# A list scheduler that makes gate products and table making own their destination slot first

## The chip, the cores and the metric

The kernel runs on the 8 cores of one Trainium2 chip. The metric is the device time of the slowest core, in microseconds (us). Most executions of one kernel agree within 0.3% (fast runs). There is a second, slower state, in which the cores of one die show a lower granted TensorE clock; such runs are called slow and are left out of every comparison here.

PE is TensorE's matmuls, PEld its weight loads, DVE is VectorE, ACT is ScalarE, POOL is GpSimd and SP is SyncE.

## The reference

One inference step of a 4-layer decoder trunk, on 8 prompts of 2048 tokens and 128 single-token samples. Cut to what matters:

```python
def _layer(x, ...):
    h = rmsnorm(x);  z = h @ w_in                 # zb, zc, zv, zu, ga, gs
    conv_out, _ = conv_causal(zc * zv, ...)       # "convolution products": zc, zv, zb
    ya = zb * conv_out
    ys, hr, hi = s5(zu, ...)                      # diagonal state-space scan
    gy = gelu(ys)
    ys = gy * sigmoid(gy @ w_glu + b_glu)         # "GLU products"
    m = sigmoid(ga) * (ya @ wb1) + sigmoid(gs) * (ys @ wb2)   # "gate products": ga, gs
    x = x + m @ w_out
    x = x + (silu(h2 @ w_gate) * (h2 @ w_up)) @ w_down
```

Each core takes one prompt, in two halves, and a share of the samples. The scan is done with tables of powers of the state's eigenvalues, in four scan groups per layer. The tables are made on DVE, ScalarE and GpSimd while the first half of a layer is being worked on. The second half loads the saved tables. Making a table is a long chain of elementwise work with two sines in it.

## The kernel before

Nothing is scheduled on the chip. A Python list scheduler with a model of the five engines fixes each engine's instruction order beforehand. Tiles live in pools of few slots; the pools that matter here are:

```python
    PP = Pool("psum", 8, lambda s: PSUM[s], reserve=3)        # the eight PSUM banks
    TP = Pool("tb", 4, lambda s: TB[:, s, :], reserve=-1)     # "TB rows": sigmoid(gate); also scratch of table making
    TABP = Pool("tab", 2, lambda s: TAB[:, s, :], reserve=-1) # a finished scan table
```

An operation may be picked when its inputs are ready and when every tile that it uses has a slot, or can get one:

```python
        def feasible(o, t):
            need = {}
            for tl in o.tiles:               # every tile that a read or write key of o names
                if tl.slot is None:
                    need.setdefault(tl.pool, []).append(tl)
            for p, tls in need.items():
                free = p.free
                if len(free) < len(tls):
                    return False
                ...                          # reserve, and turns in order for reserve=-1
            return True
```

A gate product is eight matmuls into a PSUM bank; a ScalarE sigmoid then empties the bank into a TB row:

```python
        def gas(j4):
            uga = [next_unit("ga") for _ in range(2)]
            for jj in range(4):
                t_ = tj[jj] = TP.new()
                for blk in blks:
                    pg = projh(uga[jj // 2], jj % 2, blk)      # takes a PSUM bank
                    act(lambda e, ...: e.activation(out=t_[...], in_=pg[...], func=AF.Sigmoid),
                        [(pg,)], [(t_, blk.i)], blk.n, tset="sig")   # takes the TB row
```

Here lies what the change is about. The product names only the bank. So it can run, and fill a bank, while the row that the sigmoid needs is still held by table making. Then the bank is blocked until the row is free.

## Time and profile before

| | before |
|---|---|
| time, median of 3 runs | 3663.6 us (3660.78 to 3669.47) |
| profiled span, slowest core | 3663.7 us (cores 3647.5 to 3663.7) |
| PE busy | 3504.0 us, 96% |

PE is busy for 96% of the span and carries 88% of the chain. A reordering can only win back PE's idle time, about 160 us. Only the first two slices, one in the middle and the last fall below nine tenths. The stretches table of the slowest core (busy us of each engine, instruction counts in brackets, then granted clock, DMA share, GB/s) shows where:

```profile
...
core 3: us, PE busy (x) PEld busy (x) DVE busy (x) ACT busy (x) POOL busy (x), PEclk, DMA share, GB/s
...
90.00:140.00 50.00, 20.57 (x244) 13.31 (x246) 45.44 (x67) 18.29 (x34) 15.32 (x13) 0.65 0.35 101
140.00:160.00 20.00, 19.09 (x322) 14.58 (x316) 8.42 (x13) 17.01 (x30) 4.35 (x5) 0.85 0.54 81
160.00:200.00 40.00, 39.42 (x392) 26.59 (x393) 25.07 (x57) 15.70 (x33) 2.11 (x4) 1.00 0.63 141
...
```

From 90 to 140 us, in layer 0's first half, PE works 20.57 of 50 us and DVE 45.44. The reading of that hole comes from PE's timeline (start, length, group; in square brackets the idle time before it and what ended it). L669 with H is a projection such as a gate product, L895 and L908 belong to table making, L1080 begins a scan group's output products, L1033 begins a scan group, and L669 with R at 195 us are the GLU products:

```profile
...
91.44 1.46 PE L669 MATMUL ps<-H,RING 128*128 128x384 bf16 x8
...
95.43 1.46 PE L669 MATMUL ps<-H,RING 128*128 128x384 bf16 x8
...
106.94 0.58 PE L895 MATMUL ps<-IDB,SC 128*128 128x128 bf16 x4 [5.79 <-ACT TAB L775]
...
111.34 2.72 PE L669 MATMUL ps<-H,RING 128*128 128x384 bf16 x8
...
128.63 0.58 PE L895 MATMUL ps<-IDB,SC 128*128 128x128 bf16 x4 [5.96 <-ACT R L775]
...
140.61 0.27 PE L1080 MATMUL ps<-UU,TAB 128*128 128x128 bf16 x1
...
160.14 0.67 PE L1033 MATMUL ps<-UU,TAB 128*64 128x64 bf16 x31
...
195.26 0.98 PE L669 MATMUL ps<-R,RING 128*128 128x384 bf16 x5
```

and ScalarE's timeline (L1158 is a gate's sigmoid, L775 and L776 are the two sines of a table):

```profile
...
137.80 1.28 ACT L1158 ACT_TABLE_LOAD   x1
139.09 1.93 ACT L1158 ACTIVATE TB<-ps 128x384 f32<-128x384 f32 x5
...
149.07 0.42 ACT L775 ACTIVATE TAB<-SC 128x256 f32<-128x256 f32 x1
...
155.84 1.49 ACT L1158 ACTIVATE TB<-ps 128x272 f32<-128x272 f32 x4
157.34 1.28 ACT L776 ACT_TABLE_LOAD   x1
158.64 0.51 ACT L776 ACTIVATE TAB<-SC,CST 128x256 f32<-128x256 f32 x1
...
```

Between the last of the sigmoids here (they end at 157.33) and the second sine (158.64) ScalarE runs an ACT_TABLE_LOAD of 1.28 us; the switch took about 1.30 us in all.

Five gate products run at 91.44, 95.43, 98.8, 99.7 and 111.34 us (the third and the fourth are in lines left out). All five sigmoids run in one group at 139.09, just after table making gave up the rows. So five of the eight banks lay blocked for 26 to 46 us. What else needed PE in that time (the convolution products, scan group 1's output products) waited for banks. Three banks were left, and often free, but `reserve=3` (in the lines of `feasible` left out above) keeps the last three for the tile whose turn it is in the program, and that was one of table making or of the scan. A rerun of the scheduler shows these products refused with three banks free. So five blocked banks closed PSUM to all other work. The group at 111.34 also shows the clock: eight matmuls took 2.72 us there, against 1.46 for the same product at 91.44. A gap of 5.79 us ends at 106.94, not 5 us ahead of the slow product; the clock record of this core drops to half at 104.85 us, inside that gap, and stays there until 145.81, so that the mean granted clock of this stretch is 0.65.

### The profile page before, as it was taken

Reading aid. Unit: us, or ns where it says so; the run is one execution under the profiler, and the core shown is the slowest. Engines: PE = TensorE matmul, PEld = TensorE weight load, DVE = VectorE, ACT = ScalarE, POOL = GpSimd, SP = SyncE. Lnnn points to the kernel's source line nnn. Section 1 sums busy time; section 2 is a strip of 40 time slices with the busy share of each in tenths; the row PEclk is TensorE's granted clock in tenths of the full one; section 3 lists DMA queues with packets and bytes.
Section 4 is the critical chain, followed back from the end, with each engine's and each line's share of the span. In section 5 each row is a group of like instructions: output and inputs, shape, how many; then the busy total and the mean of one; then the engine's idle time right before and its main releaser. Section 6 shows DMA issues by size and latency. Waiting matters only on the chain.

```text
span 3663.7 us, 67385 instructions; the slowest of 8 cores (3647.5 to 3663.7 us)
## 1 busy us (share of the span) xinstructions
PE 3504.0 (96%) x23912; PEld 1979.7 (54%) x23912; DVE 1618.6 (44%) x2889; ACT 1141.7 (31%) x2151; POOL 608.7 (17%) x799
## 2 busy tenths in 40 slices
PE   6699999999999999999999899999999999999998
PEld 3466666666666666666664344444444444444443
DVE  8745555465454654543244331354224442254313
ACT  4443234332353322533134320243103421042202
POOL 4232210322103221030000200002000110002000
PEclk9799999999999999999999999999999999999999
DMA  7444557435574355854338544574445644474443
GB/s 157 115 82 70 114 139 149 87 66 113 138 155 86 62 113 135 185 110 84 70 71 196 116 77 71 98 169 74 75 77 115 144 70 81 70 146 79 79 72 87
DMA packets 252804, 384.14 MB, mean 105 GB/s; under 512 B 157632, under 2 KB 180800, under 8 KB 246848
## 3 DMA queue, kind: packets, MB, share of 16 engines
q0 software_dynamic: 67968, 243.30, 39.5%
q1 hardware_dynamic: 184512, 136.53, 12.8%
q8 instruction: 202, 3.31, 0.4%
q14 instruction: 122, 1.00, 0.1%
HBM read 567.06 MB, written 56.12 MB: 170 GB/s over the span
## 4 chain that ended last, share of the span: by engine, by line
PE 88%; DVE 4%; issue 3%; DMA 3%; ACT 1%; SPq 1%; DVEq 0%; ACTq 0%; POOL 0%; POOLq 0%
PE ps L669 83%; DMA yT<-X 1%; PE ps L702 1%; PE ps L1107 1%; DVE SC L561 1%; DVE H L726 1%; PE ps L1033 1%; PE ps L908 1%; PE ps L1080 0%; DVE X L1246 0%; DMA scv<-CIN 0%; SPq L632 0%; PE ps L895 0%; DMA X<-xsT 0%; DVE R L1225 0%
## 5 line engine op out<-in xcount | busy, mean ns | idle before, releaser
L669 PE MATMUL ps<-H,RING 128*128 128x512 bf16 (+2 forms) x12160 | 2194.9, 340 | 23.5 <-DVE H L726 9.7
L669 PEld LDWEIGHTS ps<-H,RING 128*128 128x128 bf16 x12160 | 1191.5, 99 | 965.9 <-issue 52.3
L669 PE MATMUL ps<-R,RING 128*128 128x384 bf16 (+2 forms) x6400 | 1162.1, 339 | 19.7 <-DMA R<-dy 11.4
L669 PEld LDWEIGHTS ps<-R,RING 128*128 128x128 bf16 x6400 | 624.2, 98 | 517.8 <-issue 35.4
L656 POOL DMA_DIRECT2D RING<-wpk x472 | 253.0, 537 | 2635.0 <-PE ps L669 2431.7
L1268 DVE TENSOR_TENSOR R<-SC,ps 128x384 bf16<-128x384 f32 (+2 forms) x440 | 255.8, 583 | 786.7 <-PE ps L669 773.6
L1267 ACT ACTIVATE SC<-ps 128x384 f32<-128x384 f32 (+2 forms) x440 | 226.1, 515 | 1208.0 <-PE ps L669 1199.6
L1246 DVE TENSOR_TENSOR X<-X,ps 128x384 f32<-128x384 f32 (+2 forms) x480 | 269.8, 582 | 448.2 <-PE ps L669 445.2
L700 ACT ACTIVATE H<-X 128x384 bf16<-128x384 f32 (+2 forms) x304 | 156.6, 539 | 198.4 <-DVE X L1246 178.7
L726 DVE SCALAR_TENSOR_TENSOR H<-X,PRM,SC 128x384 bf16<-128x384 f32 (+2 forms) x304 | 183.0, 672 | 35.0 <-ACT SC L707 34.8
L1240 POOL TENSOR_TENSOR R<-TB,SC 128x384 bf16<-128x384 f32 (+1 forms) x160 | 168.1, 1063 | 113.1 <-DVE SC L1237 101.4
L1237 DVE TENSOR_TENSOR SC<-SC,ps 128x384 f32<-128x384 f32 (+1 forms) x160 | 92.7, 584 | 163.5 <-PE ps L669 78.6
L1236 ACT ACTIVATE SC<-ps 128x384 f32<-128x384 f32 (+1 forms) x160 | 81.4, 515 | 248.2 <-PE ps L669 219.8
L1213 DVE TENSOR_TENSOR TB<-TB,ps 128x384 f32<-128x384 f32 (+2 forms) x160 | 89.9, 582 | 128.6 <-PE ps L669 124.6
L1172 DVE TENSOR_TENSOR CIN<-ps,SC 128x384 f32<-128x384 f32 (+2 forms) x80 | 47.0, 587 | 200.7 <-ACT SC L1171 192.6
L561 DVE TENSOR_TENSOR SC<-TB 128x512 f32<-128x512 f32 (+1 forms) x160 | 124.1, 785 | 8.1 <-PE ps L908 0.6
L1158 ACT ACTIVATE TB<-ps 128x384 f32<-128x384 f32 (+1 forms) x160 | 78.9, 516 | 85.8 <-PE ps L669 85.4
L702 PE MATMUL ps<-H,ONESB 128*128 128x384 bf16 (+2 forms) x320 | 78.1, 348 | 27.5 <-ACT H L700 26.8
L561 POOL TENSOR_TENSOR TB<-TB 128x512 f32<-128x512 f32 (+1 forms) x72 | 89.3, 1242 | 42.3 <-DVE R L835 20.7
L1225 DVE TENSOR_TENSOR R<-R,SC 128x384 bf16<-128x384 bf16 (+2 forms) x80 | 46.4, 588 | 88.8 <-ACT SC L1223 86.7
L899 ACT ACTIVATE TAB<-ps 128x512 bf16<-128x512 f32 x60 | 35.5, 597 | 133.0 <-PE ps L895 132.8
L1171 ACT ACTIVATE SC<-ps 128x384 f32<-128x384 f32 (+2 forms) x80 | 41.0, 513 | 95.7 <-PE ps L669 95.5
(180 smaller groups left out, 1633.1 us busy)
## 6 DMA issues: line engine op xcount, KB each, us to landing
RING<-wpk POOLq DMA_DIRECT2D x440, 512.0 KB, 7.0
TAB<-stash SPq DMA_DIRECT2D x21, 1792.0 KB, 10.0
stash<-TAB SPq DMA_DIRECT2D x15, 1792.0 KB, 7.6
R<-stash SPq DMA_DIRECT2D x7, 1792.0 KB, 14.8
RING<-wpk POOLq DMA_DIRECT2D x32, 384.0 KB, 6.1
du<-R SPq DMA_DIRECT2D x32, 256.0 KB, 9.2
UU<-du SPq DMA_DIRECT2D x32, 256.0 KB, 7.2
dy<-YY SPq DMA_DIRECT2D x32, 256.0 KB, 6.6
```

Source lines behind the costliest of these rows:

```text
L561: fn = lambda e: e.tensor_tensor(out=out(), in0=a(), in1=b(), op=op)
L656: S.dma("pool", lambda e: e.dma_start(out=t[:, 0:n], in_=wpk[l, ui, :, 0:n]), [("X",) + gate] if gate else (), [(t,)], 128 * n * 4, prio=- ...
L669: subs.append((lambda e, u=u, kw=kw, c=c, src=src, i=i: e.matmul(ps[:, 0:blk.n], lhsT=u.ap(kw, c), rhs=src(blk), start=(i == 0), stop=(i = ...
L700: act(lambda e, kt=kt: e.activation(out=hq(kt), in_=xin(kt)[0], func=AF.Square), xin(kt)[1], qkeys(kt, blk), n)
L702: S.pe([(lambda e, kt=kt: e.matmul(ps[:, 0:n], lhsT=ONESB[:], rhs=hq(kt), start=(kt == 0), stop=(kt == 7)), qkeys(kt, blk) + [C_("ONESB")] ...
L726: dve(lambda e, kt=kt, xi=xi, g=g: e.scalar_tensor_tensor(out=H[:, kt, blk.c0:blk.c0 + n], in0=xi(), scalar=g, in1=rs[:, 0:n], op0=ALU.mul ...
L1213: dve(lambda e, po=po, n=n, t_=t_, blk=blk: e.tensor_tensor(out=t_[:, blk.c0:blk.c0 + n], in0=t_[:, blk.c0:blk.c0 + n], in1=po[:, 0:n], op ...
L1237: dve(lambda e, sg=sg, po=po, n=n: e.tensor_tensor(out=sg[:, 0:n], in0=sg[:, 0:n], in1=po[:, 0:n], op=ALU.mult), [(sg,), (po,)], [(sg,)], n)
L1240: S.op(MENG, lambda e, sg=sg, n=n, t_=t_, blk=blk, j=j: e.tensor_tensor(out=R[:, MT[j], blk.c0:blk.c0 + n], in0=t_[:, blk.c0:blk.c0 + n], ...
L1246: dve(lambda e: e.tensor_tensor(out=X[:, j, blk.c0:blk.c0 + n], in0=X[:, j, blk.c0:blk.c0 + n], in1=ps[:, 0:n], op=ALU.add), [(ps,)] + xke ...
L1267: act(lambda e, sg=sg, pg=pg, n=n: e.activation(out=sg[:, 0:n], in_=pg[:, 0:n], func=AF.Silu), [(pg,)], [(sg,)], n, tset="silu")
L1268: dve(lambda e, sg=sg, pu=pu, n=n, blk=blk, ti=ti: e.tensor_tensor(out=R[:, ti, blk.c0:blk.c0 + n], in0=sg[:, 0:n], in1=pu[:, 0:n], op=ALU ...
```

## The change

The gate product and the first DVE multiply of a table get an extra read key on their destination tile. Nothing ever writes that key, so it makes no dependence, no semaphore and no wait on the chip. It only makes the tile one of the operation's tiles, so that `feasible` asks for the TB row (or TAB slot) before the operation may take a bank (or scratch).

```diff
-    def proj(parts, blk):
+    def proj(parts, blk, own=()):
...
-                [u.key] + keys(blk), MMN(blk.n)))
+                [u.key] + keys(blk) + list(own), MMN(blk.n)))
...
-    def projh(u, mt, blk):
-        return proj([...], blk)
+    def projh(u, mt, blk, own=()):
+        return proj([...], blk, own)
...
-                tt(zz1, ..., ALU.mult, bkk, [(z1,)], 512)
+                tt(zz1, ..., ALU.mult, bkk + [(tab, "own")], [(z1,)], 512)
...
-                    pg = projh(uga[jj // 2], jj % 2, blk)
+                    pg = projh(uga[jj // 2], jj % 2, blk, [(t_, "own")])
```

More of the change, by code (lines that the diff above doesn't have):

```diff
@@ L79 @@
     LAT = 0.07
+    LATPE = 0.07
     SWITCH = 1.28
@@ L332, in schedule @@
                 s.npred -= 1
-                r = o.end + (0.0 if e == "pe" and s.eng == "pe" else self.LAT) - s.offs[i]
+                r = o.end + (0.0 if e == "pe" and s.eng == "pe" else self.LATPE if s.eng == "pe" else self.LAT) - s.offs[i]
                 if r > s.ready:
@@ L685, in rk @@
         return lambda blk: rkeys(t, blk)
-    def projh(u, mt, blk):
-        return proj([(u, k, mt * 128, hsrc(k), hk(k)) for k in range(8)], blk)
+    def projh(u, mt, blk, own=()):
+        return proj([(u, k, mt * 128, hsrc(k), hk(k)) for k in range(8)], blk, own)
     def projr(u, c, slots, blk):
@@ L864, in prep_f @@
                 o8 = 8 * h
-                tt(zz1, lambda: Bv(me, 0), lambda o8=o8: Pv(pw, o8), ALU.mult, bkk, [(z1,)], 512)
+                tt(zz1, lambda: Bv(me, 0), lambda o8=o8: Pv(pw, o8), ALU.mult, bkk + [(tab, "own")], [(z1,)], 512)
                 tt(zz2, lambda: Bv(bct, 256), lambda o8=o8: Pv(me, 512 + o8), ALU.mult, bkk, [(z2,)], 512)
```

## The prediction

> **What bounds the kernel now.** TensorE. The page shows PE busy 3504 of 3663.7 us (96%), granted clock 0.98, and PE as 88% of the chain that ended last. PE idles some 160 us in all, the bound for any reordering. The largest hole (stretches table): in 90 to 140 us PE is busy 20.6 of 50 us, while DVE is busy 45.4 (making layer 0's scan tables).
>
> **What the change does.** It adds no work and no wait on the chip. A list scheduler orders the kernel beforehand; the "own" key makes an operation eligible only once its destination slot (a TB row for a gate product, a TAB slot for a table's first multiply) is free. Only order changes.
>
> **Where it acts.** I matched each of 160 gate products in the trace with the ScalarE sigmoid that empties its bank. Long holds occur twice:
> 1. Layer 0, first half: five gate products run at 91.4 to 114 us, their sigmoids at 139.1 to 141.0, because table making holds all four TB rows until 137 to 140. Five of eight PSUM banks lie blocked 26 to 46 us each.
> 2. Second half's start: eight gate products at 1955.8 to 1969.7 hold all banks until 1974.5 to 1978 (PE idle 5.5 us). Rows are late because output stores are (yT<-X took 17 to 19 us to land), which the scheduler doesn't foresee: its plan has the rows free. I expect no change there.
>
> For tables I expect nothing: GpSimd's half of each table takes the TAB slot well ahead of the DVE multiply that must now own it.
>
> **What place 1 is worth.** With five banks blocked, scan group 1's output products ran at 140.6, though their last input was ready at 114.6; the convolution products behind the gates (18 of about 1.3 us, weights issued by 84 us) ran at 157 to 182. Late gelus and sigmoids split the last table's two sines: 149.1 and 158.6 us, input ready at 143.7. That held the last scan group until 160.1, and the GLU products until 195.
>
> PE gaps from 91 to 147 sum to about 27 us. Afterwards convolution products and scan group 1 should fill them, and gate products (16 us) run at about 137 to 155. Against this: five gate products (7 us) no longer fill holes, and DVE, nearly saturated until 137, carries about 12 us of convolution work earlier, delaying the last table a few us. I estimate 8 to 20 us saved, carried unchanged through PE-bound layers, with a few us of ripple either way: about 13 us, 0.35%.
>
> **Prediction.** 3650 us, range 3635 to 3664. Chances: faster 0.01, within 2% 0.98, slower 0.01.
>
> **What would show it.** No gate product before about 135 us in layer 0, sigmoids within 3 us of them; scan group 1's output products near 115; PE busy over 30 us in 90 to 140; last scan group before 155; layer 1 begins 8 to 20 us earlier and the lead stays constant. [...]
>
> **What would make it wrong.** Convolution products block banks in the gates' stead, waiting for DVE (gain near 0); the freed PE time reappears as a wait for GLU inputs at 175 to 195; or the new order carries worse table switches or DMA collisions into later layers.

## More of the kernel before

The page of the kernel before, first its span, then PE's busy time, then two rows of 40 slices (tenths busy, and tenths of full clock), the queue that fetches instructions, and the engines' shares of the chain that ended last:

```profile
span 3663.7 us, 67385 instructions; the slowest of 8 cores (3647.5 to 3663.7 us)
...
PE 3504.0 (96%) x23912; PEld 1979.7 (54%) x23912; DVE 1618.6 (44%) x2889; ACT 1141.7 (31%) x2151; POOL 608.7 (17%) x799
...
PE   6699999999999999999999899999999999999998
...
PEclk9799999999999999999999999999999999999999
...
q8 instruction: 202, 3.31, 0.4%
...
PE 88%; DVE 4%; issue 3%; DMA 3%; ACT 1%; SPq 1%; DVEq 0%; ACTq 0%; POOL 0%; POOLq 0%
...
```

## The result, and the profile after

| | before | after |
|---|---|---|
| fast runs, us | 3660.78, 3663.6, 3669.47, 3660.88 | 3657.23, 3654.7, 3662.24 (one more, 3778.43, was slow) |
| ratio of fast runs | | 0.9985, 95% interval 0.9963 to 1.0006 |
| profiled span (cores) | 3663.7 (3647.5 to 3663.7) | 3655.6 (3641.9 to 3655.6) |
| PE busy | 3504.0 | 3504.5 |
| PE busy, 90 to 140 us | 20.57 | 34.13 |

A ratio, here and below, is the mean time of one kernel's fast runs over that of the other's of the same rounds. It is therefore not quite the ratio of the medians that are quoted. The same program was run once more under the name of an experiment (e2 below): 0.9988, 0.9975 to 1.0001. Both intervals include 1, so the timed runs alone show no gain; their middle values are 0.12 to 0.15%, some 5 us. The profiles do show one: the cores of two profiles of this program (after and e2) end at 3648.5 and 3648.9 us in the mean, those of two of the program before (before and e1) at 3655.9 and 3656.3. The slowest core ends 8.1 us earlier.

The page after, the same lines:

```profile
span 3655.6 us, 67351 instructions; the slowest of 8 cores (3641.9 to 3655.6 us)
...
PE 3504.5 (96%) x23912; PEld 1977.8 (54%) x23912; DVE 1617.2 (44%) x2889; ACT 1139.4 (31%) x2150; POOL 609.4 (17%) x799
...
PE   6899999999999999999999899999999999999998
...
PEclk9899999999999999999999999999999999999999
...
q8 instruction: 202, 3.31, 0.4%
...
```

Work is unchanged, the span is shorter, and one digit of PE's row and of the clock's row in the second slice rose. The stretches:

```profile
...
90.00:140.00 50.00, 34.13 (x459) 22.27 (x452) 49.09 (x79) 22.37 (x44) 13.96 (x11) 0.78 0.42 112
140.00:160.00 20.00, 19.40 (x220) 13.31 (x219) 15.99 (x26) 13.55 (x26) 6.64 (x7) 0.96 0.66 116
160.00:200.00 40.00, 37.72 (x380) 24.51 (x379) 20.91 (x46) 19.47 (x38) 5.54 (x9) 1.00 0.63 130
...
```

PE does 13.6 us more between 90 and 140, at a mean granted clock of 0.78 instead of 0.65. PE's timeline after (all line numbers are one higher):

```profile
...
92.18 1.09 PE L670 MATMUL ps<-H,RING 128*128 128x272 bf16 x8
...
96.19 1.18 PE L670 MATMUL ps<-H,RING 128*128 128x272 bf16 x8
...
100.13 7.19 PE L670 MATMUL ps<-H,RING 128*128 128x384 bf16 x32
...
110.79 6.23 PE L670 MATMUL ps<-H,RING 128*128 128x272 bf16 x32
...
125.87 0.22 PE L1081 MATMUL ps<-UU,TAB 128*128 128x128 bf16 x1
...
148.37 14.27 PE L670 MATMUL ps<-H,RING 128*128 128x384 bf16 x96
...
165.68 0.67 PE L1034 MATMUL ps<-UU,TAB 128*64 128x64 bf16 x31 [1.52 <-ACT CIN L1179]
...
187.62 2.58 PE L670 MATMUL ps<-R,RING 128*128 128x384 bf16 x16
```

The products from 92 to 117 us are now convolution products; the gates come at 148.37 and later. Scan group 1's output products came at 125.87 (before 140.61), but the last scan group only at 165.68 (before 160.14). The GLU products came at 187.62 (before 195.26). Two more views say why the scan did not gain. DVE's timeline, L1173 being the multiply that empties the banks of a convolution product:

```profile
...
115.83 0.43 DVE L1173 TENSOR_TENSOR CIN<-ps,SC 128x272 f32<-128x272 f32 x1
...
116.78 0.55 DVE L1173 TENSOR_TENSOR CIN<-ps,SC 128x384 f32<-128x384 f32 x1
...
```

DVE is busy for 49.09 of the 50 us, mostly with tables, so these multiplies, which empty the banks that were filled from 92 us on, wait until 115.83. The convolution products hold the banks in the gates' place, though for a shorter time (12 to 26 us between a product's end and the multiply that empties its bank, against 26 to 46 for the five gates). ScalarE's timeline, L776 and L777 being the two sines of the last table, L900 a copy of that table from PSUM:

```profile
...
156.17 0.42 ACT L776 ACTIVATE TAB<-SC 128x256 f32<-128x256 f32 x1
...
157.90 1.55 ACT L1159 ACTIVATE TB<-ps 128x384 f32<-128x384 f32 x4
159.47 1.28 ACT L777 ACT_TABLE_LOAD   x1
160.76 0.51 ACT L777 ACTIVATE TAB<-SC,CST 128x256 f32<-128x256 f32 x1
...
164.57 0.65 ACT L900 ACTIVATE TAB<-ps 128x512 bf16<-128x512 f32 x1
...
```

The gates' sigmoids now stand between the last table's two sines (156.17 and 160.76), and more of them stand ahead of its copy at 164.57. After the change the gates are not early, but they still meet the last table on ScalarE.

To follow the gain through the program I matched every scheduled operation with its record in the trace, in order. Two cores of each profile have some matmul records missing, so the figures are means of the six complete cores. "Lead" is the time by which the kernel after is ahead at the end of a stage, in us:

```
end of                    layer 0 GLU  layer 0 w_out  layer 2 GLU  layer 3 GLU  2nd half, l.0  2nd half, l.1  end
lead of after over before     8.2          11.3           7.5          5.0          6.3            7.4        7.4
```

The order of the two programs differs in layer 0's first half (47 PE, 31 ScalarE and 52 DVE operations have other places, and 3 on ScalarE in layer 1). After that the order is the same on every engine, though not the slots: which bank, which slot of the weight ring and which scratch row a tile gets differs to the end of the program. Yet a third of the lead of 11.3 us is gone by the end. Of the 11.3 us, 3.1 are won between layer 0's GLU products and its w_out (86.4 us after, 89.5 before). The later stages of large products (SwiGLU and so on) agree within 0.2 us between before and after, and within 1.0 us in all profiles; what varies is the scan stages, from the scan inputs to the GLU products. Their lengths, for later use, also from the matching, with the end of the program:

```
                   first half: layer             second half: layer        mean
                     0     1     2     3          0     1     2     3       end
before             152.7 104.1 102.8 102.2      117.3  94.8  97.2  85.6   3656.0
after              144.2 104.2 106.6 104.9      115.8  93.7  97.1  85.9   3648.5
e1 tables only     152.4 104.3 102.9 103.2      117.0  94.9  97.0  86.1   3656.7
e2 gates only      144.5 103.9 106.8 104.5      116.8  93.5  98.0  85.9   3650.0
e3 hostage         152.0 105.8 103.2 102.4      114.2  94.0  98.5  87.3   3662.1
e4 dump            141.7 104.7 106.9 103.8      115.9  94.2  97.8  85.9   3647.7
e5 after + 10      144.9 104.9 104.0 102.4      115.5  94.0  96.6  85.8   3644.6
e6 before + 246    151.3 104.5 106.3 104.3      115.2  93.5  96.7  85.9   3668.0
e7 after + 138     143.7 103.1 102.8 104.3      116.6  93.0  92.6  87.6   3642.1
e8 after, late     145.6 104.4 107.0 103.9      110.7  93.0  98.0  85.9   3645.7
e9 before, late    152.3 105.0 103.7 102.5      113.1  94.4  97.5  86.2   3656.2
e10 late + 138     145.2 103.7 102.9 104.3      112.0  92.7  93.0  88.4   3642.1
e11 late + 202     144.3 103.4 103.7 106.4      109.8  96.7  93.4  85.5   3647.2
```

### The profile page after: what moved, and what is told of

Same layout as the page of the kernel before. It is cut to its first block, busy times and chain, and to the rows that moved or that the text cites. A ratio compares the mean times of both kernels' runs of the same rounds, so it can differ in the third digit from the quotient of the medians.

```text
span 3655.6 us, 67351 instructions; the slowest of 8 cores (3641.9 to 3655.6 us)
## 1 busy us (share of the span) xinstructions
PE 3504.5 (96%) x23912; PEld 1977.8 (54%) x23912; DVE 1617.2 (44%) x2889; ACT 1139.4 (31%) x2150; POOL 609.4 (17%) x799
## 4 chain that ended last, share of the span: by engine, by line
PE 88%; DVE 4%; issue 3%; DMA 3%; ACT 1%; SPq 1%; DVEq 0%; ACTq 0%
PE ps L670 84%; DMA yT<-X 1%; PE ps L703 1%; PE ps L1108 1%; DVE H L727 1%; DVE SC L562 1%; PE ps L1034 1%; PE ps L909 1%; PE ps L1081 0%; DMA scv<-CIN 0%; DVE X L1247 0%; SPq L633 0%; PE ps L896 0%; DVE R L1226 0%; DMA X<-xsT 0%
## 5 line engine op out<-in xcount | busy, mean ns | idle before, releaser
L1238 DVE TENSOR_TENSOR SC<-SC,ps 128x384 f32<-128x384 f32 (+1 forms) x160 | 92.9, 584 | 160.8 <-PE ps L670 83.0
L1173 DVE TENSOR_TENSOR CIN<-ps,SC 128x384 f32<-128x384 f32 (+2 forms) x80 | 46.9, 587 | 184.5 <-ACT SC L1172 165.8
L900 ACT ACTIVATE TAB<-ps 128x512 bf16<-128x512 f32 x60 | 35.4, 597 | 126.9 <-PE ps L896 126.8
```

Source lines behind the costliest of these rows:

```text
L1238: dve(lambda e, sg=sg, po=po, n=n: e.tensor_tensor(out=sg[:, 0:n], in0=sg[:, 0:n], in1=po[:, 0:n], op=ALU.mult), [(sg,), (po,)], [(sg,)], n)
```

## The experiments

Eleven kernels in three batches, each batch on one chip with the kernel before beside it (its medians, slow runs included: 3664.14, 3664.80 and 3668.73 us). The theory: blocked banks in layer 0 are the whole cause, and the gates' half of the change does it all. Rivals: the tables' half does it; or a luckier order does it, whatever the banks do.

### Batch 1: which half, and is it the banks?

**e1, the tables' half alone.** The gate call goes without its list, the rest is the change.

```diff
-                    pg = projh(uga[jj // 2], jj % 2, blk, [(t_, "own")])
+                    pg = projh(uga[jj // 2], jj % 2, blk)
```

> Only the table half of the change (the first multiply of each table must own its TAB slot), gates as before. The instruction order and the slots on every engine come out the same as in the kernel before. Theory A (the table half does nothing): ratio 1.000 within 0.2%; all stages of the profile within their run-to-run spread of before. Rival (table half carries part of the gain): ratio near 0.998 and the layer 0 hole in 90 to 140 us filled. This run is also a second profile of the kernel before, and so measures how much the stage lengths of layers 1 to 7 vary from run to run with nothing changed.

Measured: 1.001, 0.9997 to 1.0022. The scheduler gives the same order and the same slots as for the kernel before, so this is also a measure of the noise: 0.1% between identical programs. The tables' half does nothing: in the scheduler's plan GpSimd's part of the table has taken the TAB slot before the DVE multiply asks for it in 13 of 16 tables, and in the other three the slot is free when the multiply asks.

**e2, the gates' half alone.** On the kernel after, the tables' key is taken out.

```diff
-                tt(zz1, ..., ALU.mult, bkk + [(tab, "own")], [(z1,)], 512)
+                tt(zz1, ..., ALU.mult, bkk, [(z1,)], 512)
```

> Only the gate half of the change. Order and slots come out the same as in the changed kernel. Theory A (the gate half is all of it): ratio about 0.998 (-5 to -9 us), lead of about 11 us over before at the output projection of layer 0. The lead in the changed kernel's profile fell from 11.3 us (layers 0 and 1) to 7.5 in layer 2's scan stage and 5.0 in layer 3's, though the order there is that of before. If that loss is chance of one run, it will be elsewhere or absent here; if it belongs to the program (theory F: where the instruction stream's blocks fall, which 10 fewer PE instructions shifted), layer 2's scan stage is again about 106.5 us against 102.8.

Measured: 0.9988, 0.9975 to 1.0001. The order is that of the kernel after; it is a second sample of the same program. Its lead at layer 0's output projection is 10.7 us, and its scan stage of layer 2 is again long, 106.8 us: the lead that is lost later was not chance of one run.

**e3, banks blocked on purpose.** On the kernel after, five tiny products take a bank each at the time of the gates, and ScalarE empties them into the first gate's TB row, so only when that row is free. Nothing else is undone: the gates still own their rows. It is five matmuls of 64 columns and five small copies of added work.

```diff
                 t_ = tj[jj] = TP.new()
+                for i_ in range(5 if hs and l == 0 and j4 == 0 and jj == 0 else 0):
+                    ph = PP.new()
+                    S.pe([(lambda e, ph=ph: e.matmul(ph[:, 0:64], lhsT=IDB[:], rhs=IDB[:, 0:64], ...), [...], MMN(64))], [(ph,)], FULL)
+                    act(lambda e, t_=t_, ph=ph: e.activation(out=t_[:, 0:64], in_=ph[:, 0:64], func=AF.Copy), [(ph,)], [(t_, 0)], 64)
```

> The changed kernel, but in layer 0 five one-matmul products take a PSUM bank where the five early gate products did, and their banks are emptied only when the first TB row comes free; right results. Theory A (five blocked banks are what held the convolution products and scan group 1 back): PE in 90 to 140 us falls back to 15 to 22 us busy, the 11 us lead at layer 0's output projection is lost, and since the gates' own 7 us of work no longer fills the hole the kernel is 0 to 8 us slower than before, ratio 1.000 to 1.002. Rival B (the gain comes from the gates' later place in the order, not from the banks): lead of 8 to 11 us stays, ratio about 0.998.

Measured: 1.006, 1.0023 to 1.0097 (fast runs 3668.67 to 3702.38). The stretches of its slowest core:

```profile
...
90.00:140.00 50.00, 15.75 (x241) 11.72 (x242) 46.13 (x69) 16.91 (x35) 15.32 (x13) 0.53 0.35 100
...
```

With five banks blocked again, PE falls back from 34.13 to 15.75 of 50 us, below the kernel before. Layer 0's scan stage is back at 152.0 us (after 144.2, before 152.7), and its output projection ends at 297.3 us (before 291.7, after 280.4). So blocked banks alone take the gain away, and more, with every gate owning its row. It is lower than before, probably because five gate products (7 us of work) no longer fill the hole. The rival of a luckier order, whatever the banks do, falls. (The scheduler answers the blocked banks with another order, so banks and order can't be parted further than that.) The timed loss is larger than the profile's: its mean end is 6.1 us, 0.17%, above before's, while the timed runs say 0.6% and scatter more than those of any other kernel. The record shows why. Two of the five fast runs (3691.18 and 3702.38) count as fast, but one die of theirs is 15 and 29 us longer than the other at a lower clock (0.978 and 0.973 against 0.982): a mild form of the slow state. Die 0, undisturbed in all five, ends at 3661.7 us (median of its cores, mean of the runs), against 3653.7 in the fast runs of before, so the loss is some 8 us, 0.2%.

**e4, banks freed without moving the gates.** On the kernel before, layer 0's first-half sigmoids write to a spare tile at once, so early gates block nothing; the later multiply reads that tile. The result is wrong on purpose (one tile for all gates).

```diff
+                    if hs and l == 0 and j4 == 0:
+                        act(lambda e, ...: e.activation(out=DUMP[:, 0:blk.n], in_=pg[:, 0:blk.n], func=AF.Sigmoid), [(pg,)], [C_("DUMP")], ...)
+                        continue
```

> The kernel before, but layer 0's first gates are written to a spare 128x384 buffer (wrong results on purpose), so the gate products can run early and their banks are emptied at once, without the change. Theory A (banks): PE in 90 to 140 us is busy over 34 us, as gates (16 us) and convolution products both fill it; the lead at layer 0's output projection is 11 us or more, 12 to 20, ratio 0.994 to 0.998. Rival B (gates must come late): no gain, ratio about 1.000. Rival C (the early stage is bound by DVE's table making whatever PE does): gain at most that of the change, with the last scan group no earlier than 160 us.

Measured: 0.9982, 0.9968 to 0.9996. The stretches, and two lines of PE's timeline, of its slowest core:

```profile
...
90.00:140.00 50.00, 38.58 (x481) 26.00 (x478) 41.28 (x64) 30.96 (x55) 13.93 (x13) 0.86 0.56 120
140.00:160.00 20.00, 13.02 (x184) 8.41 (x184) 16.67 (x29) 8.17 (x18) 5.99 (x6) 0.99 0.28 62
160.00:200.00 40.00, 34.53 (x330) 22.33 (x324) 20.97 (x48) 13.78 (x28) 1.61 (x4) 0.92 0.67 135
...
```

```profile
...
159.61 0.95 PE L1034 MATMUL ps<-UU,TAB 128*64 128x64 bf16 x31 [2.87 <-ACT TAB L939]
...
190.50 8.11 PE L670 MATMUL ps<-R,RING 128*128 128x384 bf16 x41 [4.67 <-DMA R<-dy]
...
```

PE is busy 38.58 of the 50 us, more than after, though the gates keep their early place. The lead at layer 0's output projection is 13.4 us (after 11.3). The rest of the freed time comes back as new waits. From 140 to 160 us PE is busy for 13.0 to 14.9 of the 20 us on all eight cores (before 19.09), and its longest wait there, 2.87 us in front of the last scan group, ends with that group's table (L939), although no sigmoid stands between the table's two sines any more. From 160 to 200 this slowest core alone also waits 4.67 us for the DMA that brings the GLU inputs, and so has 34.53 of 40 us; the other seven cores have 38.2 to 39.2 (before 39.42), without that wait. So the limit behind the banks is the last table, whose DVE work ends at about 155 us (core 1), mixed with convolution work on the same engine, and on seven of eight cores not the GLU inputs. I take from it that no order of the gates is likely to be worth much more here; that is inferred from this one order.

### Batch 2: where did a third of the lead go?

The layer-2 and layer-3 scan stages are 3.8 and 2.7 us longer after than before, with the same order. Two things differ: the slots of the tiles, and PE's program, which is 10 instructions shorter by then (semaphore instructions 3977 before, 3967 after). Theory: PE's instruction stream comes in blocks, and where a block ends among tiny scan matmuls, PE starves. Shifting the stream by 10 instructions moves these ends. Rivals: the other slots, or other timing of DMA or DVE work; the padding below changes neither order nor slots.

The page's queue q8 has 202 instruction packets of 16,384 bytes each, and PE's 23,912 matmuls, 23,912 weight loads and 3977 semaphore instructions make 51,801, which is 202 times 256 and a rest. So I take a block to be one packet with 256 of PE's instructions, an estimate from these counts. Whether the ends of blocks cost PE time is what the next three runs test.

**e5 and e7: the kernel after with 10 and 138 more PE instructions; e6: the kernel before with 246 more** (which equals 10 fewer, modulo 256). The instructions are waits at the very start for a count that is soon reached:

```diff
+            for k_ in range(N if e == "pe" else 0):           # N = 10, 138 or 246
+                eng.wait_ge(sems["dve"], 1)
             for o in self.order[e]:
```

> The changed kernel with 10 harmless, long satisfied waits in front of TensorE's instructions, so that from layer 1 on its instruction stream stands where it stood in the kernel before (the change had taken out 10 TensorE instructions). Theory F (the lead lost in the scan stages of layers 2 and 3 comes from where blocks of the instruction stream end, not from order or data): layer 2's scan stage returns from 106.6 to 102.8 within 0.5 us, layer 3's from 104.7 to 102.2 to 103.2, and the lead at the end grows from 7 to 11 to 13 us, ratio 0.9965 to 0.998. Rival N (slot assignment or timing of the other engines, which the pad doesn't touch): layer 2's stage stays at 106.6 and the ratio at 0.9987.

> The kernel before with 246 harmless waits in front of TensorE's instructions: 246 is 10 short of 256, the block that the trace shows (instruction fetches of 16384 bytes). Order and slots are untouched. Theory F: layer 2's scan stage grows from 102.8 to 106.6 within 0.5 us and layer 3's from 102.7 to about 104.7, as in the changed kernel; the end is 4 to 7 us later than before, ratio about 1.0015. Rival N: the stages stay at 102.8 and 102.7, ratio 1.000.

> The changed kernel with 138 harmless waits: half a block away from the place of the kernel before. Theory F: the scan stages of several layers differ by 1 to 5 us from both kernels' values, in either direction, while the stages of large products (230.2, 25.3, 209.3, 22.8 us) stay within 0.2 us. Rival N: all stages as in the changed kernel within 0.5 us.

Measured: e5 0.9967, 0.9953 to 0.9981. e6 1.0034, 1.0016 to 1.0052. e7 0.9961, 0.9947 to 0.9975. With 10 useless instructions the kernel after gets its layer-2 and layer-3 stages back, 104.0 and 102.4 us (a little above expectation in layer 2); with 246 the kernel before gets the long ones of after, 106.3 and 104.3. So the slots are not the cause. (In the rounds of this batch two fast runs of the kernel before, 3680.82 and 3676.05, have one die 17 and 9 us longer than the other at a lower clock, as in e3. Without them the plain ratios of means are 0.9972 for e5, 1.0037 for e6, 0.9966 for e7 and 0.9976 for e8.) The end of e6 was mis-expected: the 246 instructions cost 10.4 us at the start (its first stage starts at 60.0 instead of 49.6), which nothing hides.

The same stretch of layer 2 on core 1, in PE's timeline. Before:

```profile
...
1061.75 0.20 PE L1097 MATMUL ps<-AS0Z,TAB 128*128 128x16 bf16 x2 [4.28 <-issue]
...
```

After:

```profile
...
1052.88 0.17 PE L1094 MATMUL ps<-UU,TAB 128*128 128x16 bf16 x1 [3.59 <-issue]
...
1059.31 1.03 PE L1108 MATMUL ps<-VT,TAB 64*128 64x64 bf16 x59
1062.38 0.24 PE L1108 MATMUL ps<-VT,TAB 64*128 64x64 bf16 x5 [2.03 <-issue]
...
```

e5, after with 10 more instructions:

```profile
...
1051.30 0.19 PE L1100 MATMUL ps<-AS0Z,TAB 128*128 128x16 bf16 x2 [2.89 <-issue]
...
1058.02 1.11 PE L1110 MATMUL ps<-VT,TAB 64*128 64x64 bf16 x64
...
```

Before has one hole in this stretch, ended by "issue": no wait that the profile shows. After has a second, which cuts a group of 64 matmuls (L1108) after the 59th; in e5 that group is whole again (x64). Then I listed, for all eight cores of all 13 profiles, every gap over 1.2 us between two matmuls of the same scheduled operation with no semaphore instruction in front of the second (where a core misses records the matching is off by some places, which leaves the gap but not its number), and set it beside the landings of q8's instruction packets. Core 1, the numbers being where PE resumed, the gap (from start to start of the two matmuls, so some 0.2 us more than the idle time in the timelines above), the record's number modulo 256 among PE's instructions, and the time since the last landing:

```
before   599.51 4.07 188 1.37 | 1061.75 4.45 187 1.42 | 1528.14 2.34 187 1.45 | 2846.38 3.52 187 1.42 | 3251.17 1.58 188 1.47
after    591.65 5.17 188 1.55 | 1052.88 3.76 187 1.48 | 1062.38 2.22 187 1.50 | 1523.77 1.74 188 1.51 | 1534.15 1.79 187 1.39
         2829.63 2.38 188 1.57 | 2856.24 1.66 187 1.34 | 3259.45 1.64 188 1.39
e5       590.12 4.61 188 1.44 | 1051.30 3.06 187 1.26 | 1519.25 2.62 187 1.53 | 2840.44 3.52 187 1.32 | 3245.52 1.86 188 1.39
e7       591.08 1.93 188 1.49 | 597.83 1.76 187 1.55 | 1040.95 1.46 187 1.18 | 1059.69 1.92 188 1.61 | 1512.77 3.93 188 1.35
```

All stand at one place of the 256 (187 or 188), and in all PE resumed 1.2 to 1.6 us after an instruction block had landed. On the six complete cores of all 13 profiles every one of 442 holes stands at 187 to 189; the 26 of e11 stand at 187 or 188, as its expectation asked. Over all cores and profiles 580 of 583 holes resumed 1.0 to 1.8 us after a landing. Holes with a semaphore in front, such as those of the GLU products at about 2032 us, come at other places and 0.5 to 16 us after a landing. The theory holds: these are instruction fetches that come late. Their sum, as a mean of the eight cores, accounts for the lost lead:

```
              holes  sum, us                   holes  sum, us
before         4.9    15.0      after           6.9    19.2
e1             4.8    15.1      e2              7.4    19.5
e3             4.4    13.5      e4              7.1    20.4
e6 (+246)      6.8    18.7      e5 (+10)        4.4    14.7
                                e7 (+138)       5.1    12.3
e9             5.6    18.3      e8              6.2    18.1
                                e10             5.0    12.0
                                e11             4.4    12.9
```

After carries 4.2 us more of these holes than before; the lead lost between layer 0 and the end is 11.3 - 7.4 = 3.9 us. e5 has 4.5 us fewer than after and ends 3.9 us earlier; e7 has 6.9 us fewer and ends 6.4 us earlier.

**e8, the scheduler told of late stores.** The other place of blocked banks that the prediction named, the start of the second half, is untouched by the change, because the scheduler does not know how late the output stores land (medians of 16.6 and 19.4 us from issue to landing there, before). Here the kernel after is told, by 15 us more in its model of these stores; the work is the same, the order differs.

```diff
-                      [k_ for k_ in xik if k_[2] != 8], [], 128 * npr * 4)
+                      [k_ for k_ in xik if k_[2] != 8], [], 128 * npr * 4, extra=15.0)
```

> The changed kernel, with 15 us more landing time told to the scheduler for the stores of the first half's output (they took 17 to 19 us where it reckoned 2), so that at the start of the second half the gate products' rows count as late and the own key acts there too. If blocked banks cost time at place 2 as at place 1 (theory A2): the hole of 5.5 us near 1970 us goes, the first scan group there runs before 1983 us instead of 1987, and the scan stage of the second half's first layer falls from 116 to 117 us to 108 to 113; ratio about 0.9965. Rival (that stage is bound by the DMA chain of the scan, du, UU and dy, whatever the banks do): the stage stays within 2 us of 116, the hole moves to the wait for R<-dy near 2033 to 2043.

Measured: 0.9972, 0.9956 to 0.9987. The stage is 110.7 us (after 115.8, before 117.3). On the six complete cores its first scan group starts 36.4 to 37.6 us into the stage, instead of 45.0 to 52.5 (after), and the wait of 8 to 11 us for the GLU inputs, which all six show after, is gone from all six. The key works there too, once the model shows the row to be taken.

### Batch 3: knowledge without ownership, and both together

**e9, the same on the kernel before**, so that the scheduler knows of the late stores but no gate owns its row.

```diff
-                      [k_ for k_ in xik if k_[2] != 8], [], 128 * npr * 4)
+                      [k_ for k_ in xik if k_[2] != 8], [], 128 * npr * 4, extra=15.0)
```

> The kernel before (no own key) with the same 15 us of landing time told to the scheduler: the control for the run of the changed kernel with late stores. The scheduler now sees the rows as late but may still run gate products ahead of them, and plans five of them so. Theory A2 (the own key is what frees the banks at place 2): the scan stage of the second half's first layer stays at 114 to 118 us, ratio 0.9995 to 1.001. Rival (knowing of the late stores is enough, because it moves the scan groups ahead of other products): the stage is 108 to 112 us as with the key, ratio about 0.9985.

Measured: 0.9977, 0.9945 to 1.0008. The stage is 113.1 us, between the two expectations. So knowing gives 4.2 us (117.3 to 113.1), and ownership some 2.4 more (113.1 to 110.7; e10 and e11, with e8's order, have 112.0 and 109.8); neither theory was right alone. That the second step is more than scatter (the six cores of e9 lie between 109.2 and 115.4) shows in what the key acts on: in e9 the first scan group starts 39.9 to 44.4 us into the stage, and all six cores still wait 4 to 9 us for the GLU inputs, where e8 has no such wait. At the end e9 keeps nothing (3656.2 against 3656.0 us), and 3.3 us more of late fetches (18.3 against 15.0) would account for most of that.

**e10 and e11, late stores with 138 and 202 more PE instructions**, on the kernel after.

```diff
+            for k_ in range(N if e == "pe" else 0):           # N = 138, 202
+                eng.wait_ge(sems["dve"], 1)
...
+                      ..., 128 * npr * 4, extra=15.0)
```

> The changed kernel with the late stores told and with the 138 waits: both findings together. If they add: layer 2's scan stage 102.8, layer 6's 92.6, the second half's first 110 to 112; mean span of the profile's cores 3635 to 3640 against 3656 before; ratio 0.9940 to 0.9955, faster than either kernel. If the late-store order moves TensorE's instructions by 3 and that undoes the good place of the second half: 3640 to 3645.

> The same with 202 waits: another place of the instruction blocks. Theory F: scan stages of layers 1 to 7 differ from those with 138 waits by 1 to 5 us in either direction, large products' stages within 0.2 us, and every hole over 1.2 us inside a group of products without a wait again stands at one and the same place modulo 256 instructions (records 187 or 188). Ratio 0.994 to 0.998.

Measured: e10 0.9948, 0.992 to 0.9976; e11 0.997, 0.9938 to 1.0002. This batch was noisy: of eleven runs of the kernel before, four were slow, and another took 3689.94 us, with one die 20 us longer than the other at a lower clock. Without that run the plain ratios are 0.9959 for e10 and 0.9981 for e11. e10 has the lowest ratio and e7 (0.9961) the second; in their profiles both end before both kernels and cannot be told apart: the mean end is 3642.1 us in both (after 3648.5, before 3656.0). The expected sum of the two gains (3635 to 3640) was missed. e10 won 4.6 us over e7 in the second half's first scan stage (116.6 to 112.0) and had lost or lost again 1.5 us in layer 0 and 0.8 in the last layer; the rest I have not accounted for. Its late-fetch holes sum to 12.0 us, about e7's 12.3, so they are not where it went. e11's scan stages differ from e10's by up to 4.0 us, in both directions, as the theory of the blocks has it.

## Why the prediction was right or wrong

3657 us lies in the range, but the range, up to 3664, took in the kernel before as well, so it would have held with no gain at all; what tests the prediction is its steps. The cause named, blocked banks in layer 0, is shown by e3 (blocking alone takes the gain back) and e4 (freeing alone gives it). "For tables I expect nothing" is shown by e1, and "no change" at the second half's start is borne out (117.3 to 115.8 us, with the wait for rows still there). Point by point:

- *PE busy over 30 us in 90 to 140*: right, 34.13. *Layer 1 begins 8 to 20 us earlier*: right, 11.3.
- *No gate product before about 135 us*: right in sense, 148.4. The estimate of "about 137 to 155" was early: DVE, with convolution work moved ahead, freed the rows at 147.2 instead of 137.3. *Sigmoids within 3 us of them*: wrong, up to 4.7 us between a product's end and its sigmoid, because they share ScalarE with the last table's sines and with five ACT_TABLE_LOADs of 1.28 us each (149.91 to 161.59).
- *Scan group 1's output products near 115*: wrong, 125.9. The prediction had named why among its doubts: convolution products block banks in the gates' stead, waiting for DVE (92 to 115.8 us).
- *Last scan group before 155*: wrong, 165.7, later than before's 160.1. The prediction took "late gelus and sigmoids split the last table's two sines" for a harm that the change would cure. The sigmoids still split them, 156.2 and 160.8. In e4, where nothing splits them, the last scan group still comes only at 157 to 160 us, after DVE's work on the last table.
- *That held … the GLU products until 195*: the step fails in its cause. They came 7.6 us earlier although the last scan group was 5.5 us later (slowest core of each; the mean lead of six cores at this point is 8.2). PE is nearly full from 147 us on in both kernels (19.1 of 20 us and 39.4 of 40 before, 37.7 of 40 from 160 after), and no wait stands before their first line in either timeline, so what held the GLU products was PE work in front of them. Part of that work moved into the hole, and that is the gain. That the gain at layer 0 (11.3 us) came out near the forecast is partly luck, since this half of the reasoning did not hold. When the chain does bind, one sees it as on the slowest core of e4: 34.53 of 40 us.
- *Carried unchanged through PE-bound layers, with a few us of ripple*: this is the term that mis-sized the total. The gain at layer 0 (11.3 against "about 13") was near; 3.9 us were given back later, and the runs show to what: 4.2 us more of late instruction fetches, from a program that is 10 instructions shorter. The order in these layers, the stages of large products (within 0.2 us) and the busy time did not change.

What stays open: why e10 does not add e7 and e8, what triggers a fetch (at the holes of core 1 the packet starts only some 2.2 to 2.7 us before PE resumes, and takes 0.9 to 1.2 us), and what happens in the 1.4 us between landing and resuming.

## What to carry to other kernels

An operation that fills a scarce buffer should be held back until the place that it is drained to is free; otherwise it turns a wait on an idle engine into blocked buffers for the busy one. The number of banks was not the cause here, the order in which they were given out was: with the same eight banks PE went from 20.57 to 34.13 of 50 us. A pure reordering is worth what the busiest engine's hole can take, so count what else can run in the hole, and what else will hold the same buffers, before counting chains behind it. When two programs of the same order differ by a few us, look where bursts of tiny instructions stand in the instruction stream before inventing a cause (a scan group here is 152 matmuls and as many weight loads in about 3.6 us of PE's time). Late fetches showed here as gaps put down to "issue" (1.5 to 5.2 us in the core-1 list), at one place modulo 256 of PE's instruction count (187 to 189), 1.0 to 1.8 us (in 580 of 583 cases) after a packet of 16,384 bytes of the instruction queue had landed, 12 to 20 us of them in all per execution (means of eight cores). 10 harmless instructions moved the mean end by 3.9 us (0.1%; the intervals of the timed ratios, 0.9967 for e5 and 0.9985 for after, overlap) and 138 by 6.4 us (0.2%), and 246 lengthened the stages that 10 had shortened. The next edit that shifts the stream can undo such a gain. And look at the clock of each die in every run before explaining a scatter: at least five runs counted as fast here were disturbed.
